# Rope transposes, gate stores, score banks, y tiles, zero tile and raw tiles of y in a two-layer hybrid backbone

## The chip, the cores and the metric

The kernel runs on one core of a Trainium2 chip. The metric is the time of one execution on the device in microseconds (us). Engines are named as in the profile: PE (matmul), PEld (its weight loads), DVE (VectorE), ACT (ScalarE), POOL (GpSimd) and SP (SyncE, which here issues most DMA transfers, in order).

## The reference

Two layers over 1024 latent tokens and 256 context tokens (1280, in ten chunks of 128), model width 1024, all in fp32. Layer 0 runs sixteen neighbourhood-attention heads beside four bidirectional mLSTM heads of width 256, with one input and one output projection. Layer 1 has sixteen bidirectional HGRN2 heads. Each layer is modulated by `c`.

```python
for l in range(DEPTH):
    shift, scale, gate = _ada(c, w_ada[l], b_ada[l])
    h_lat = _rms(x, norm_w[l]) * (1.0 + scale) + shift
    if l % 2 == 0: y_lat, y_ctx = _ab_mixer(...)   # attention heads || mLSTM heads
    else:          y_lat, y_ctx = _c_mixer(...)    # HGRN2 heads
    x = x + gate * y_lat

# mLSTM, one chunk (forward and backward over the chunks)
s   = einsum(q, k) * exp(dmat - m_t)                # scores, decayed
num = einsum(s, v) + carry_w * einsum(q, C)
den = sum(s) + carry_w * einsum(q, n)
h   = num / maximum(abs(den), exp(-m_t))
C   = dec * C + einsum(k * exp(g - m_new), v)       # state; n likewise
# merge, then the output projection
hb  = _rms(hb * sigmoid(ob), h_norm);  yb = hb * silu(zb)
y   = concatenate([ya, yb]) @ w_out
```

q and k of the mLSTM heads are rotated by an axial rope table.

## The kernel before

**Arithmetic.** Each fp32 operand of a dense product is split into a high and a low part: ACT casts the high part (L74), DVE subtracts for the low one (L75), and each product is three matmuls (L127 to L129, in the output projections L771 to L773). PE bounds most stages.

**Order.** The program is written in the Tile framework. A scheduler orders each engine's instructions by its own model of their times; work marked as filler goes in where an engine is thought free, and `issue_after` ties the issue of a DMA to another instruction. Each engine then works through its row of instructions in order, and a tile (a buffer of a tag with so many copies) is written again only when its last reader is done. PSUM has two "mm" and two "tr" banks for the whole program, and further ones for a phase: in the mLSTM recurrence two "s" and two "acc".

**Stages** (times in the trace): norm and modulation to about 50 us; values of the first attention heads to 80; `rope_tables`, `ml_gates`, the modulation of layer 1 and the q projections of two mLSTM heads (`q_plain_t`) to 190; projections done ahead to 420; attention to about 1313; the mLSTM recurrence to 1725, with output-projection pieces (`out_some`) and gate projections as filler; the rest of layer 0's output projection to 1850; layer 1's projections to 2200, its heads to about 3240, its output projection to the end.

**The places that the change touches.**
- `rope_tables` loads the rope rows (SP), transposes them with four small matmuls (L1045, L1046) and copies the result with six ACT instructions. `ml_gates` follows: it loads the gate weights `wgr`, copies them (`wgw`, DVE L329), projects (L347, three groups, each transposed by L354), runs the gate scans on DVE (L382 to L395, ending in `gR` and, by transposes at L403, `gcol`), and stores Gd and mpd and loads mpb back, five DMAs on SP (L408 to L413).
- `wblock` loads a weight slab in pieces of a raw tile `wraw` (L103) and splits each (L74, L75).
- In the recurrence (`ml_all`) `ml_load` loads a chunk, transposes k in a "tr" bank (L434), copies it to mkT (ACT L436), and later computes scores in an "s" bank (L441), copied to mST (ACT L443). A step makes the numerator in "acc" (L496, L506) and two state updates u in the "s" banks (L513), which DVE adds to the state mC (L521, 128x258). `ml_out` transposes a finished chunk of y by two matmuls in a "tr" bank (L560), scales it into `myt` (ACT L561) and stores it by POOL.
- `out_y` loads y for a token tile in two raw tiles (L760, tag `wraw`, three copies, shared with weights) and splits them; `out_tile` multiplies and adds bias, gate and residual on DVE (L805, L807, L808), with `oxh` loaded by SP at L795.
- At the start of layer 0's last projection a zero tile `gzero` is set by DVE (L1500); its first use is in layer 1's heads.

## Time and profile before

| | |
|---|---|
| median of three runs | 3443.36 us (3441.47 to 3443.4) |
| the profiled execution | 3451.55 us, its span 3449.8 us |
| granted PE clock, mean | 0.995 |
| PE waits of the trace, sum | 37 us, and 5.2 us before the first matmul, 3.8 us after the last |

A row of waits reads: the engine, the bank or tile and line that waited, what it waited for, and the total, times and longest. A row of the timeline reads: start and length in us, engine, line, operation, out<-in; in brackets how long the engine stood idle before it, and for what. A window row gives each engine's busy time in a stretch, then the granted clock of PE.

### The profile page before, as it was taken

The numbers are of one execution on the slowest core, as the hardware profiler recorded it, in microseconds if no ns is written. First come the engines' busy times: TensorE is split into PE (matmuls) and PEld (weight loads), VectorE is DVE, ScalarE is ACT, GpSimd is POOL, SyncE is SP. The second block draws the span as 40 slices with busy tenths as digits, with TensorE's granted clock in tenths as the row PEclk, the third lists the DMA queues.
The fourth block names the chain that finished last, engine by engine and source line by source line (L and its number), as shares of the span: only waits on it lengthen the run. The fifth ranks groups of instructions, "written<-read, shape, count | busy, mean of one in ns | idle before, by whom it ended". The sixth has DMA issues, their size and how long they took to land. (4 is left out here: it accounts for less than half of the span.)

```text
span 3449.8 us, 62306 instructions
## 1 busy us (share of the span) xinstructions
PE 3403.7 (99%) x23360; PEld 3065.3 (89%) x23360; DVE 2349.8 (68%) x5814; ACT 1495.6 (43%) x3469; POOL 498.2 (14%) x834
## 2 busy tenths in 40 slices
PE   8999999999999999999999999999999999999999
PEld 5689999999999999987879998899999999999887
DVE  5577757666666654666678666577777777777855
ACT  5322245555544534555546323444444444444431
POOL 3111212222222211211212111000000000000010
PEclk9999999999999999999999999999999999999999
DMA  8543422232223225464473332211111111111345
GB/s 270 185 134 109 127 63 72 69 96 73 81 76 87 77 89 164 143 184 146 137 252 130 110 105 92 77 41 62 53 49 54 61 53 50 56 61 51 114 149 169
DMA packets 359517, 359.62 MB, mean 104 GB/s; under 512 B 30584, under 2 KB 304184, under 8 KB 359088
## 3 DMA queue, kind: packets, MB, share of 16 engines
q1 hardware_dynamic: 315248, 246.36, 24.2%
q0 software_dynamic: 43824, 109.16, 9.2%
q8 instruction: 184, 3.01, 0.4%
q14 instruction: 117, 0.96, 0.1%
q10 hardware_dynamic: 144, 0.13, 0.0%
HBM read 271.98 MB, written 83.42 MB: 103 GB/s over the span
## 5 line engine op out<-in xcount | busy, mean ns | idle before, releaser
L129 PE MATMUL mm<-hh,wl 128*128 128x512 f32 (+1 forms) x1564 | 567.7, 363 | 2.7 <-DVE wl L75 2.7
L127 PE MATMUL mm<-hh,wh 128*128 128x512 f32 (+1 forms) x1564 | 564.3, 361 | 0.3 <-ACT ev L1072 0.2
L128 PE MATMUL mm<-hl,wh 128*128 128x512 f32 (+1 forms) x1564 | 563.9, 361 | 0.0
L127 PE MATMUL mm<-wh,hh 128*128 128x256 f32 x1880 | 541.4, 289 | 1.3 <-ACT wh L74 1.2
L129 PE MATMUL mm<-wh,hl 128*128 128x256 f32 x1880 | 541.7, 289 | 0.2 <-DVE hl L75 0.2
L128 PE MATMUL mm<-wl,hh 128*128 128x256 f32 x1880 | 541.2, 288 | 0.5 <-DVE wl L75 0.3
L127 PEld LDWEIGHTS mm<-wh,hh 128*128 128x128 f32 x1880 | 358.3, 191 | 5.3 <-issue 2.6
L129 PEld LDWEIGHTS mm<-wh,hl 128*128 128x128 f32 x1880 | 358.7, 191 | 4.4 <-issue 2.4
L128 PEld LDWEIGHTS mm<-wl,hh 128*128 128x128 f32 x1880 | 358.6, 191 | 3.0 <-DVE wl L75 1.0
L127 PEld LDWEIGHTS mm<-hh,wh 128*128 128x128 f32 x1564 | 295.6, 189 | 44.2 <-issue 5.1
L129 PEld LDWEIGHTS mm<-hh,wl 128*128 128x128 f32 x1564 | 295.2, 189 | 42.6 <-DVE wl L75 3.1
L128 PEld LDWEIGHTS mm<-hl,wh 128*128 128x128 f32 x1564 | 295.6, 189 | 38.6 <-issue 1.7
L74 ACT CAST wh<-wraw 128x512 fp32r<-128x512 f32 x292 | 179.7, 621 | 266.2 <-PE mm L128 156.9
L1212 ACT COPY gksel<-gK 128x512 f32<-128x512 f32 x224 | 148.6, 664 | 276.9 <-PE s L1221 265.2
L75 DVE TENSOR_TENSOR wl<-wraw,wh 128x512 fp32r<-128x512 f32 x292 | 197.3, 684 | 55.4 <-ACT wh L74 52.8
L1221 PE MATMUL s<-gQ,gksel 128*128 128x128 f32 x1536 | 202.1, 276 | 0.0
L1221 PEld LDWEIGHTS s<-gQ,gksel 128*128 128x128 f32 x1536 | 192.6, 191 | 5.8
L771 PE MATMUL mm<-woh,yh 128*128 128x512 f32 (+1 forms) x420 | 169.8, 404 | 4.9 <-DVE oacc L805 2.5
L773 PE MATMUL mm<-woh,yl 128*128 128x512 f32 (+1 forms) x420 | 164.6, 393 | 0.9 <-DVE yl L75 0.9
L772 PE MATMUL mm<-wol,yh 128*128 128x512 f32 (+1 forms) x420 | 165.3, 394 | 0.0
L1242 DVE TENSOR_TENSOR gQ<-gQ,gT 128x256 f32<-128x256 f32 x384 | 143.1, 413 | 21.2 <-PE s L1221 21.2
L1234 DVE COPY_PREDICATED gA<-glm,s 128x512 f32<-128x512 uint8 x160 | 117.2, 733 | 55.8 <-PE s L1221 55.8
(590 smaller groups left out, 7981.7 us busy)
## 6 DMA issues: line engine op xcount, KB each, us to landing
wraw<-in_wc_dram SPq DMA_DIRECT2D x130, 256.0 KB
wraw<-yd SPq DMA_DIRECT2D x128, 256.0 KB
wraw<-in_wab_dram SPq DMA_DIRECT2D x98, 256.0 KB
md<-ev POOLq DMA_DIRECT2D x78, 256.0 KB, 2.7
adar<-in_wada_dram POOLq DMA_DIRECT2D x16, 1024.0 KB, 6.0
b<-in_wc_dram SPq DMA_DIRECT2D x62, 256.0 KB
adar<-in_wada_dram SPq DMA_DIRECT2D x16, 512.0 KB
wraw<-in_wab_dram SPq DMA_DIRECT2D x64, 128.0 KB
```

The source lines that it names most:

```text
L74: nc.scalar.copy(hi, x)
L75: nc.vector.tensor_tensor(out=lo, in0=x, in1=hi.bitcast(F32), op=ALU.subtract)
L127: mm(ps, lhsT=lh(k), rhs=rh(k), start=(first and k == 0), stop=False)
L128: mm(ps, lhsT=lh(k), rhs=rl(k), start=False, stop=False)
L129: mm(ps, lhsT=ll(k), rhs=rh(k), start=False, stop=(last and k == nk - 1))
L771: mm(ps, lhsT=yh[:, k, :], rhs=w.h(k)[:, cols], start=(k == 0), stop=False)
L772: mm(ps, lhsT=yh[:, k, :], rhs=w.l(k)[:, cols], start=False, stop=False)
L773: mm(ps, lhsT=yl[:, k, :], rhs=w.h(k)[:, cols], start=False, stop=(k == 7))
L1212: nc.scalar.copy(ksel.rearrange("p (b s i) -> p b s i", s=2, i=h), pick(K))
L1221: nc.tensor.matmul(pa[:, c, :].rearrange("p (b s i) -> p b s i", s=2, i=h), lhsT=ksel[:, c * P : (c + 1) * P], rhs=qp[:, c * nbc : (c + 1) ...
L1234: nc.vector.copy_predicated(A, self.lmask[:, lev - 1, :].unsqueeze(1).to_broadcast([P, 4, P]), pa)
L1242: nc.vector.tensor_tensor(out=t[:, i, :, s, :], in0=t[:, i, :, s, :], in1=bc(tot), op=ALU.mult)
```

## The change

Six edits; the matmuls and all other computing instructions are the same in number and kind.

1. `rope_tables` returns a function `turn`, and `ml_gates` calls it after its three projection groups, so the four transposes and six copies come later.
2. `ml_gates` returns a function `store` for the five DMAs of Gd, mpd and mpb. It is called after both `q_plain_t`, with an issue tied to the last weight load.
3. The scores of the mLSTM heads go to the "tr" banks, leaving the "s" banks to the state updates.
4. `myt` has three copies in place of two.
5. `out_y` takes tag and copies of its raw tiles: four `wraw` in layer 0's last projection (the early weights of layer 1 there share them), and six `yraw` of their own in the tail of layer 1.
6. `gzero` and its memset move to the opening of the pool of layer 1's heads.

```diff
@@ -100,7 +100,7 @@
             off = 0
             for s in srcs:
                 c = s.shape[1]
-                nc.sync.dma_start(
+                self.last_w = nc.sync.dma_start(
                     out=r3[:, :, off : off + c],
                     in_=s[i * step * P : (i + 1) * step * P].rearrange("(k p) f -> p k f", p=P),
                 )
@@ -319,7 +319,7 @@
         return self.proj_out(c0, dst, gate, rev)
 
 
-    def ml_gates(self, pool, keep):
+    def ml_gates(self, pool, keep, turn):
         nc, a = self.nc, self.a
         raw = self.t(pool, [P, KD, P], F32, "wgr", 1)
         nc.sync.dma_start(out=raw, in_=a["wg"].rearrange("(k p) f -> p k f", p=P))
@@ -361,6 +361,7 @@
                 nc.scalar.activation(
                     dst[32:36, b0 : b0 + n], ps[q + 64 : q + 68, ::-1], AF.Identity, bias=self.bg[q + 64 : q + 68, :]
                 )
+        turn()
         tmp = self.t(pool, [36, T], F32, "gt", 1)
 
         nc.vector.scalar_tensor_tensor(out=tmp, in0=gf, scalar=-1.0, in1=gf, op0=ALU.mult, op1=ALU.max)
@@ -404,14 +405,18 @@
             p4 = p.rearrange("p m (d x) -> p m d x", x=32)[:, :, :, 0:4]
             nc.vector.tensor_copy(self.gcol[:, c : c + m], p4[:, :, 0:2])
             nc.scalar.activation(self.thr[:, c : c + m], p4[:, :, 2:4], AF.Exp, scale=-1.0)
-        for d in range(2):
-            nc.sync.dma_start(out=self.Gd[d], in_=GG[32 * d : 32 * d + 4, :])
-            nc.sync.dma_start(out=self.mpd[d], in_=mp[32 * d : 32 * d + 4, 0:NT])
         self.mpb = self.t(keep, [P, 2, 4, NT], F32, "mpb", 1)
-        nc.sync.dma_start(
-            out=self.mpb.rearrange("p d h c -> p (d h c)"),
-            in_=self.mpd.rearrange("d h c -> (d h c)").partition_broadcast(P),
-        )
+
+        def store():
+            for d in range(2):
+                nc.sync.dma_start(out=self.Gd[d], in_=GG[32 * d : 32 * d + 4, :])
+                nc.sync.dma_start(out=self.mpd[d], in_=mp[32 * d : 32 * d + 4, 0:NT])
+            nc.sync.dma_start(
+                out=self.mpb.rearrange("p d h c -> p (d h c)"),
+                in_=self.mpd.rearrange("d h c -> (d h c)").partition_broadcast(P),
+            )
+
+        return store
 
 
     def ml_slot(self, h, tt, n):
@@ -436,7 +441,7 @@
         nc.scalar.copy(kT, p)
 
         def score():
-            s = self.ps("s", [P, P])
+            s = self.ps("tr", [P, P])
             for j in range(2):
                 nc.tensor.matmul(s, lhsT=kT[:, j, :], rhs=st["q"][tt][:, j, :], start=(j == 0), stop=(j == 1))
             st["S"][tt] = self.t(pool, [P, P], F32, f"mST{sl}", 2)
@@ -555,7 +560,7 @@
         self.rsqrt(r, ss, 0.25 / 256)
         nc.vector.scalar_tensor_tensor(out=hs, in0=hs, scalar=r, in1=g["z"], op0=ALU.mult, op1=ALU.mult)
         p = self.ps("tr", [P, 2, P])
-        yt = self.t(pool, [P, 2, P], F32, "myt", 2)
+        yt = self.t(pool, [P, 2, P], F32, "myt", 3)
         for j in range(2):
             nc.tensor.transpose(p[:, j, :], hs[:, j * P : (j + 1) * P], self.ident)
             nc.scalar.activation(yt[:, j, :], p[:, j, :], AF.Copy, scale=self.hnb[:, 2 * h + j : 2 * h + j + 1])
@@ -751,11 +756,11 @@
         nc.gpsimd.dma_start(out=self.yd[p2], in_=z)
 
 
-    def out_y(self, tt, q, ysrc, yp, bufs, rp=None):
+    def out_y(self, tt, q, ysrc, yp, bufs, raws=("wraw", 3)):
         yh = self.t(yp, [P, 8, P], F32R, "yh", bufs)
         yl = self.t(yp, [P, 8, P], F32R, "yl", bufs)
         for k in range(0, 8, 4):
-            yr = self.t(rp or yp, [P, 512], F32, "wraw", 3).rearrange("p (j t) -> p j t", j=4)
+            yr = self.t(yp, [P, 512], F32, *raws).rearrange("p (j t) -> p j t", j=4)
             k0 = q * 8 + k
             self.nc.sync.dma_start(
                 out=yr, in_=ysrc[k0 : k0 + 4, :, tt * P : (tt + 1) * P].rearrange("j p t -> p j t")
@@ -1040,6 +1045,15 @@
             nc.sync.dma_start(out=v(rc)[:, :, b, :], in_=rope[0:64, :, 0, 1, :])
         self.roper = self.t(pool, [P, 2, 16], F32, "roper", 1)
         self.ropec = self.t(pool, [P, 2, 64], F32, "ropec", 1)
+
+
+        def turn():
+            self.rope_turn(rr, rc)
+
+        return turn
+
+    def rope_turn(self, rr, rc):
+        nc = self.nc
         p = self.ps("tr", [P, 2, 80])
         for i in range(2):
             nc.tensor.transpose(p[:, i, 0:16], rr[:, i * P : i * P + P], self.ident[0:16, 0:16])
@@ -1420,14 +1434,16 @@
                         self.mod_tr(0, [xts[tt], xts[tt + 1]], tt, pool, self.h_sink(tt * P))
                 self.na_values(0, w)
             with self.pp.phase(ad=2), tc.tile_pool(name="gates", bufs=1) as pool:
-                self.rope_tables(rtp, (pool, "qs", 2))
-                self.ml_gates(pool, mlk)
+                turn = self.rope_tables(rtp, (pool, "qs", 2))
+                store = self.ml_gates(pool, mlk, turn)
                 self.adab, self.adak = 2, 4
                 self.ada_gate(0, pool)
                 self.ada(1, pool)
                 self.ada_gate(1, pool)
                 for h in range(2):
                     self.q_plain_t(h)
+                with tc.issue_after(self.last_w.ins):
+                    store()
             la.close()
             with self.pp.phase(sa=4), tc.tile_pool(name="qa", bufs=1) as pool:
                 self.q_open([(0, 1), (1, 2), (3, 2)], a["wab"], (self.wp, "ev", 2), (self.wp, "wraw", 3), (pool, "qs", 2), 2)
@@ -1496,8 +1512,6 @@
             with tc.tile_pool(name="op0", bufs=2) as op, ExitStack() as wl:
                 wl1 = wl.enter_context(tc.tile_pool(name="wo1", bufs=1))
                 w1 = wo(1, 0, [(wl1, "wo", 8)] * 8)
-                self.zero = self.t(lk, [P, CTX], F32, "gzero", 1)
-                nc.vector.memset(self.zero, 0.0)
                 self.lmask = self.t(lk, [P, 6, P], U8, "glm8", 1)
                 self.lmask0 = self.t(lk, [P, P], F32, "glm0", 1)
                 self.ident8 = self.t(lk, [P, P], U8, "ident8", 1)
@@ -1525,7 +1539,7 @@
                     dma(out=xt[:, 512:D], in_=self.x1[tt * P : (tt + 1) * P, 512:D])
                     part = self.t(op, [P, 512], F32, "og", 3)
                     dma(out=part, in_=self.x1[tt * P : (tt + 1) * P, 0:512])
-                    self.out_tile(w1, 0, tt, self.out_y(tt, 1, self.yd, op, 2), self.xin(tt), xt[:, 0:512], op, part)
+                    self.out_tile(w1, 0, tt, self.out_y(tt, 1, self.yd, op, 2, ("wraw", 4)), self.xin(tt), xt[:, 0:512], op, part)
                     if tt < 8:
                         nc.gpsimd.dma_start(out=self.x1[tt * P : (tt + 1) * P, 0:512], in_=xt[:, 0:512])
                     xn = self.t(op, [P, D], F32, "nx", 2)
@@ -1539,7 +1553,7 @@
                     if tt in (5, 7):
                         k = 512 * len(early)
                         src = a["wc"][k : k + 512, 3 * 2048 : 3 * 2048 + 256]
-                        early.append(self.wblock(self.wp, "w", [src], 4, 256, op, ring=self.slabs))
+                        early.append(self.wblock(self.wp, "w", [src], 4, 256, [op, 4, "wraw"], ring=self.slabs))
 
             with l1:
                 with tc.tile_pool(name="qv", bufs=1) as pool, self.pp.phase(sa=4):
@@ -1556,6 +1570,8 @@
                 sp.close()
                 pool = l1.enter_context(tc.tile_pool(name="hg", bufs=2))
                 self.rawp = pool
+                self.zero = self.t(pool, [P, CTX], F32, "gzero", 1)
+                nc.vector.memset(self.zero, 0.0)
                 l1.enter_context(self.pp.phase(s=3, acc=1))
                 st, parts = self.hg_parts(0, pool, early)
                 for part in sum(parts, []):
@@ -1607,7 +1623,7 @@
                             part = self.t(op, [P, 512], F32, "og", 4)
                             dma(out=part, in_=self.part[tt * P : (tt + 1) * P, :])
                         if b:
-                            ys[tt] = self.out_y(tt, 1, self.yd2, *((yp, 2) if tt < 2 else (op, 6)))
+                            ys[tt] = self.out_y(tt, 1, self.yd2, *((yp, 2) if tt < 2 else (op, 6, ("yraw", 6))))
                         cuts = 0 if b or tt < 7 else 2
                         self.out_tile(w, b, tt, ys[tt], self.x1[tt * P : (tt + 1) * P], xt, op, part, cuts)
                         for c in range(max(1, cuts)):
```

The order of instructions changes over the whole of the gate, projection and mLSTM stages. Line numbers of the changed kernel are higher: L386 for L385, L393 for L392, L439, L446, L518 and L565 for L434, L441, L513 and L560, L765 and L800 for L760 and L795.

DVE in the gate stage, around the weight splits (wl) of the second q head and the last gate operations; before:

```order
L392 COPY gGG_986<-gG_960 4x1024
L394 COPY gGG_986<-gG_960 4x1024
L1026 TENSOR_TENSOR ev_1381<-ev_1381,roper_846 128x512
L385 TENSOR_TENSOR gb_957<-gb_957,gG_960 36x1280
L75 TENSOR_TENSOR wl_1422<-wraw_1424,wh_1423 128x512
L1027 TENSOR_TENSOR ev_1381<-ev_1381,qs_1383 128x512
L75 TENSOR_TENSOR wl_1428<-wraw_1430,wh_1429 128x512
L392 COPY gR_984<-gb_957 4x1024
L393 COPY gR_984<-gb_957 4x256
L394 COPY gR_984<-gb_957 4x1024
L395 COPY gR_984<-gb_957 4x256
```

and in the changed kernel:

```order
L393 COPY gGG_986<-gG_960 4x1024
L395 COPY gGG_986<-gG_960 4x1024
L1029 TENSOR_TENSOR qs_1378<-ev_1376,roper_846 64x512
L386 TENSOR_TENSOR gb_957<-gb_957,gG_960 36x1280
L1030 TENSOR_TENSOR qs_1378<-ev_1376,roper_846 64x512
L75 TENSOR_TENSOR wl_1417<-wraw_1419,wh_1418 128x512
L393 COPY gR_984<-gb_957 4x1024
L394 COPY gR_984<-gb_957 4x256
L395 COPY gR_984<-gb_957 4x1024
L396 COPY gR_984<-gb_957 4x256
L75 TENSOR_TENSOR wl_1423<-wraw_1425,wh_1424 128x512
```

The first split comes after one rope operation fewer (L1026, now L1031, stands behind), and the four gR copies stand between the first and the second split. On PE, the transposes of gR (L403, now L404) come when 6 matmuls from the first that reads the first wl are through, where it was 26.

PE in the mLSTM recurrence where two heads overlap, u in "s", y and scores; before:

```order
L506 MATMUL acc_20486<-mC_18930,mqc_20490 128x258 x2
L560 MATMUL tr_20389<-ident_75,mhs_3826_20061 128x128
L513 MATMUL s_20369<-mvw_20365,mkn_3776_19919 128x258
L441 MATMUL s_20425<-mqT_3902_20284,mkT_20291 128x128 x2
L560 MATMUL tr_20344<-ident_75,mhs_3837_20086 128x128
L560 MATMUL tr_20389<-ident_75,mhs_3826_20061 128x128
L441 MATMUL s_20430<-mqT_3907_20297,mkT_20304 128x128 x2
L513 MATMUL s_20451<-mvw_20449,mkn_3672_19599 128x258
L560 MATMUL tr_20473<-ident_75,mhs_3768_19886 128x128
L496 MATMUL acc_20583<-mv_3901_20280,mSD_20581 128x258
L506 MATMUL acc_20583<-mC_20054,mqc_20587 128x258 x2
L771 MATMUL mm_20534<-woh_20114,yh_20535 128x512
```

and in the changed kernel:

```order
L518 MATMUL s_20367<-mvw_20365,mkn_3776_19919 128x258
L518 MATMUL s_20369<-mvw_20365,mkn_3776_19919 128x258
L565 MATMUL tr_20344<-ident_75,mhs_3837_20086 128x128
L565 MATMUL tr_20389<-ident_75,mhs_3826_20061 128x128
L518 MATMUL s_20451<-mvw_20449,mkn_3672_19599 128x258
L565 MATMUL tr_20344<-ident_75,mhs_3837_20086 128x128
L518 MATMUL s_20453<-mvw_20449,mkn_3672_19599 128x258
L565 MATMUL tr_20389<-ident_75,mhs_3826_20061 128x128
L518 MATMUL s_20496<-mvw_20494,mkn_3667_19586 128x258
L446 MATMUL tr_20425<-mqT_3902_20284,mkT_20291 128x128 x2
L518 MATMUL s_20498<-mvw_20494,mkn_3667_19586 128x258
L446 MATMUL tr_20430<-mqT_3907_20297,mkT_20304 128x128 x2
```

Scores now stand in "tr"; the updates u of one more pair of steps stand in the piece, with no projection matmul between.

SP in the tail of layer 1, loads of y (L760, now L765) and of the residual (L795, now L800) around the last y tiles; before:

```order
L760 DMA wraw_38450<-yd_4_66 128x4x128
L760 DMA wraw_38488<-yd_4_66 128x4x128
L795 DMA oxh_38389<-x_7_69 128x512
L760 DMA wraw_38492<-yd_4_66 128x4x128
L795 DMA oxh_38443<-x_7_69 128x512
L760 DMA wraw_38530<-yd_4_66 128x4x128
L760 DMA wraw_38534<-yd_4_66 128x4x128
L760 DMA wraw_38572<-yd_4_66 128x4x128
L760 DMA wraw_38576<-yd_4_66 128x4x128
L795 DMA oxh_38485<-x_7_69 128x512
```

and in the changed kernel:

```order
L103 DMA wraw_38385<-in_woc_dram 128x512
L103 DMA wraw_38433<-in_woc_dram 128x512
L765 DMA yraw_38492<-yd_4_66 128x4x128
L103 DMA wraw_38439<-in_woc_dram 128x512
L765 DMA yraw_38530<-yd_4_66 128x4x128
L765 DMA yraw_38534<-yd_4_66 128x4x128
L765 DMA yraw_38572<-yd_4_66 128x4x128
L765 DMA yraw_38576<-yd_4_66 128x4x128
L800 DMA oxh_38389<-x_7_69 128x512
L800 DMA oxh_38443<-x_7_69 128x512
```

All loads of y now stand ahead of the residual tile oxh_38389 and those after it, and three weight loads among the last of them.

## The prediction

> **What bounds the kernel now.** I read the page's engine shares first, then TensorE's waits, then the windows for the granted clock, and last the timeline around single stalls.

> ```profile
> span 3449.8 us, 62306 instructions
> PE 3403.7 (99%) x23360; PEld 3065.3 (89%) x23360; DVE 2349.8 (68%) x5814; ACT 1495.6 (43%) x3469; POOL 498.2 (14%) x834
> ```

> TensorE (PE) is busy 3403.7 of 3449.8 us, so it sets the time, and the change adds and removes none of its matmuls. It can win only what PE idles (46.1 us) and what a lowered clock costs; it can lose whatever new waits the new order makes. PE's waits of over 0.1 us that bear on the change or stand beside it (line, what it waited for, total us, times, longest):

> ```profile
> PE mm L771 <- ACT yh L74: 3.9, 5, 2.2
> PE tr L239 <- DVE ntmp L249: 2.8, 3, 1.8
> PE mm L129 <- DVE wl L75: 2.7, 2, 2.5
> PE mm L771 <- DVE oacc L805: 2.5, 2, 1.6
> PE tr L560 <- ACT myt L561: 2.5, 1, 2.5
> PE s L441 <- DVE mC L521: 2.2, 1, 2.2
> PE s L441 <- ACT mST L443: 1.7, 2, 1.5
> PE mm L771 <- issue: 1.2, 1, 1.2
> PE s L441 <- ACT mkT L436: 1.0, 3, 0.4
> PE tr L1045 <- DMA qs<-in_rope_dram: 0.9, 1, 0.9
> PE mm L773 <- DVE yl L75: 0.9, 2, 0.5
> PE tr L1046 <- DMA qs<-in_rope_dram: 0.6, 1, 0.6
> PE mm L347 <- DVE wgw L329: 0.2, 1, 0.2
> ```

> The edits aim at L1045/L1046 (rope transposes), L129 behind wl (gate stage), L441 (scores, 4.9 us in all), L560 (y transposes), and L771/L773 behind oacc and yl (output projections): about 14 us of the 46. A stall can cost more than its idle time. The windows show it (start:end, length, busy us and count for PE, PEld, DVE, ACT, POOL, granted clock, DMA share, GB/s):

> ```profile
> 100.00:150.00 50.00, 47.31 (x260) 33.01 (x261) 35.28 (x64) 15.03 (x25) 8.62 (x13) 1.00 0.57 186
> 250.00:300.00 50.00, 50.00 (x357) 47.28 (x356) 46.76 (x79) 16.89 (x30) 4.14 (x7) 1.00 0.28 84
> 1400.00:1450.00 50.00, 50.00 (x340) 46.53 (x339) 33.82 (x106) 26.90 (x80) 14.71 (x36) 1.00 0.53 166
> 1450.00:1500.00 50.00, 47.45 (x252) 40.93 (x251) 37.30 (x112) 30.37 (x83) 7.18 (x20) 0.97 0.67 201
> 1550.00:1600.00 50.00, 47.58 (x224) 39.71 (x223) 33.53 (x107) 29.27 (x77) 4.91 (x16) 0.97 0.50 150
> 1600.00:1650.00 50.00, 47.27 (x222) 39.19 (x221) 31.57 (x101) 27.89 (x81) 12.81 (x31) 0.97 0.50 152
> 1650.00:1700.00 50.00, 48.10 (x230) 40.23 (x229) 35.56 (x112) 26.03 (x71) 11.06 (x21) 1.00 0.34 106
> 1800.00:1850.00 50.00, 48.16 (x275) 42.29 (x274) 42.59 (x75) 39.52 (x90) 13.18 (x21) 0.97 0.52 166
> ```

> Windows with a stall of 1.8 to 2.5 us mostly show 0.97, which is 0.03 x 50 = 1.5 us of clock lost beside the idle time; the window with 1.5 us (1650) and the one with 2.5 us in the gate stage (100) show 1.00. So I price a stall of about 2 us or more at 1.5 us on top in the mLSTM stage (1313 to 1725 us), and at nothing in the gate stage.

> [...]

> **The change, part by part.** Rope transposes: PE waits 0.9 + 0.6 for the rope rows, before the gate projections (L347). What comes next there:

> ```profile
> 82.73 0.23 DVE L329 COPY wgw<-wgr 128x128 f32<-128x128 f32 x1 [2.56 <-DMA wgr<-in_wg_dram]
> 83.11 1.48 PE L347 MATMUL mm<-hh,wgw 128*32 128x512 f32 x10 [0.22 <-DVE wgw L329]
> ```

> L347 needs wgw, which ends at 82.96 because its load lands then; SP issues that load behind the rope loads both before and after. So L347 still starts near 83.0, and the freed 1.5 us become a wait for wgw. The four transposes move into a full PE stream (0.6 us, priced below by four small matmuls of the same kind), and six ACT copies go with them. I take +0.6; bounds -0.9 (if wgr comes sooner with less beside it) and +1.5 (if the copies delay an ACT eviction that PE awaits).

> Gate stores: their five DMAs leave SP's queue until the weights of the two q heads are issued. But the 2.5 us at L129 end with VectorE, not with SP:

> ```profile
> 131.25 1.48 DVE L385 TENSOR_TENSOR gb<-gb,gG 36x1280 f32<-36x1280 f32 x1
> 132.66 0.68 DVE L75 TENSOR_TENSOR wl<-wraw,wh 128x512 fp32r<-128x512 f32 x1
> 134.57 0.69 DVE L392 COPY gR<-gb 4x1024 f32<-4x1024 f32 x1
> ```

> DVE has no idle time ahead of these; the weight split L75 stands behind L385 and the rest of the gate chain. In the new order one rope operation (0.7) leaves that place, so wl comes 0.7 sooner; but the four gR copies (two of 0.69 and two of a quarter of the columns, an estimate of 0.29 each: 1.95) now stand directly behind it, and PE has their transposes right behind the matmuls that it releases. wl ends near 132.6; gR near 134.6; PE has about six matmuls (1.3 us) between, and reaches the transposes near 133.4: a new wait of 1.2. Sum -0.7 + 1.2 = +0.5; bounds -2.5 (the stall is gone) and +3 (the second split, also behind the copies, is awaited too).

> Score bank and y tile (the mLSTM stage). The scores (L441) leave the two "s" banks, which they share with the state updates u (L513), for the two "tr" banks, which hold the transposes of k (L434) and y (L560). What frees the banks, over that stage:

> ```profile
> L521 DVE SCALAR_TENSOR_TENSOR mC<-mC,mcw,s 128x258 f32<-128x258 f32 x128 | 60.7, 480 | 33.8 <-PE s L513 27.1 <-PE acc L506 6.0
> L561 ACT ACTIVATE myt<-tr,hnb 128x128 f32<-128x128 f32 x79 | 28.0, 362 | 16.0 <-PE tr L560 12.6 <-DMA yd<-myt 3.0
> L436 ACT COPY mkT<-tr 128x256 f32<-128x256 f32 x40 | 14.7, 367 | 5.7 <-PE tr L434 5.6
> L443 ACT COPY mST<-s 128x128 f32<-128x128 f32 x40 | 10.5, 263 | 14.8 <-PE s L441 14.3
> ```

> ```profile
> 1612.80 0.38 PE L513 MATMUL s<-mvw,mkn 128*128 128x258 f32 x1
> 1613.01 0.61 PE L441 MATMUL s<-mqT,mkT 128*128 128x128 f32 x4
> 1615.80 0.37 ACT L561 ACTIVATE myt<-tr,hnb 128x128 f32<-128x128 f32 x1 [3.05 <-DMA yd<-myt]
> 1616.22 0.33 PE L560 MATMUL tr<-ident,mhs 128*128 128x128 f32 x1 [2.49 <-ACT myt L561]
> ```

> The last two rows are the y stall: ACT waits 3.05 us for the store of an older y tile, with only two such tiles; PE waits 2.49 behind it. A third tile lets ACT write at once, and nothing else in that wait is late. Gross gain 2.5 + 1.5 of clock = 4.0. The scores wait 4.9 us, and the largest of those (2.2, window 1550) also has the 0.97: 6.4. Together 10.4.

> What comes back: u keeps "s" alone, but the new order is not looser everywhere. A u spends 0.2 us a pass on PE (0.4 for two), a small matmul 0.11 (the four overlapping ones take 0.61, so 0.11 to 0.15 each). With those, I counted in both orders the places where a bank is taken again within 1.1 us of PE work after its last matmul: 18 before (14 in "s", 4 in "tr"), 18 after (10 and 8). They sit where two heads overlap, as in the piece of PE's order shown above: six u, four y transposes and two scores back to back. There PE spends some 0.65 per u, while DVE owes each 0.48 (L521) beside its other chain. By count alone all 4.9 + 1.5 would come back; but a score then no longer waits behind a u on DVE, and ACT frees its bank in 0.26 to 0.37. Between these I take 2.5 of idle and one clock loss, 4.0, so the net is -6.4. Bounds: -14.1 (nothing comes back, and the 2.2 + 1.5 around 1473, L771 behind yh, go as well) and +16 (the second rival).

> Zero tile and fourth raw tile, output projection of layer 0. In the first row below DVE stands 1.37 us in a memset that reuses memory of the last y tiles:

> ```profile
> 1733.37 0.27 DVE L1500 MEMSET gzero<- 128x256 f32 x1 [1.37 <-DMA yd<-myt]
> ```

> It moves to layer 1's pool, behind that layer's first projection. The waits of PE after it, 0.9 (oacc), 0.9 (yl) and 0.6 (a share of yh), sum to 2.4; they come from DVE being late, but some of them well after it, so I take -1.5. The 1.8 at L239 (around 1841, with clock) hangs on the norm chain, which is untouched. Bounds -5.7 (2.4 and 1.8 + 1.5 all go) and +2.4 (the new order makes as many again).

> Six raw tiles in the tail of layer 1:

> ```profile
> 3378.80 0.33 SPq L795 DMA_DIRECT2D oxh<-x  x1
> 3388.25 0.62 ACT L74 CAST yh<-wraw 128x512 fp32r<-128x512 f32 x1 [2.36 <-DMA wraw<-yd]
> 3388.90 0.69 DVE L75 TENSOR_TENSOR yl<-wraw,yh 128x512 fp32r<-128x512 f32 x1 [2.08 <-ACT yh L74]
> ```

> The last y loads are queued on SP behind an oxh load that waits until 3378.80 for an output store; so the cast starts at 3388.25, the split at 3388.90, and PE's accumulator comes free late: the 1.6 of L771 behind oacc. In the new order the y loads stand ahead of those oxh loads. The oxh loads are then later, but they are added after a tile's eight products. I take -1.6; bounds -2.8 (the 1.2 "issue" goes too) and +1 (an oxh load is now the late one). That 1.2 comes from a gate load that a pool's release holds; it stays.

> Sum: +0.6 + 0.5 - 6.4 - 1.5 - 1.6 = -8.4. The profiled execution took 3451.55 (1.75 around its span), 8.2 above the median of the three; so 3443.2 by its own clock, and 3443.36 - 8.4 = **3435** for the median.

> **The rivals.** *The stalls only form anew elsewhere:* of the mLSTM gains the y wait alone is kept (-2.5), layer 0 gives nothing, the tail -1.6, the front +1.1: -3.0, 3440.4. For it: 18 close reuses before and after. Against: scores and u no longer hold each other up.

> *Slower, by the tr banks:* kT, scores and y now share two banks, 120 tiles in place of 80. Two y tiles are transposed side by side, and while both stand half done no kT or score can start, so the chain score, mST (0.26), mSD, numerator comes late. If each of the 20 pairs (40 y tiles) cost 1.0 us (two ACT evictions of 0.36 and one mST), and four of the waits a clock loss of 1.5, that is 26 against gross gains of 10.4 + 2.0: +13.6, 3457. It decides once new waits pass 12.4 + 6.9, about 19 us. For it: in the new order y pairs stand open across some 25 rows. Against: ACT is busy 27 of 50 us there, and the window at 1400 has no PE idle at all.

> *All of it goes:* mLSTM -14.1, layer 0 -5.7, tail -1.6, front 0: -21.4, 3422. Against it: the close reuses, and the norm chain.

> *The front part does not do what it says* (wgw and DVE bind, not rope and SP): that is in the forecast already.

> **How the numbers follow.** A measurement of this kernel tells no less than about 0.2% (6.9 us, below 3436.5 or above 3450.3). Forecast 0.42 (0.36 of it faster, 0.06 same), stalls anew 0.20 (0.15 same, 0.05 slower by some more of them), tr banks 0.24 (slower), all gone 0.14 (faster). That makes faster 0.50, same 0.21, slower 0.29. The forecast's own range is 3429 to 3440; with "all gone" below and most of the "tr banks" above it becomes 3420 to 3453.

> **What would show it.** Right: no L1045 wait at 80 but about 1.9 before L347; a wait of PE at 133 to 135 for gR or wl; no L560 wait for myt; L441 rows gone and a few u or score waits of 1 to 2 us where heads overlap, with at least one window of 0.97 fewer between 1313 and 1725; no DVE wait in the memset; no PE gap near 3390. Wrong: L441, L434 or L560 waits behind ACT that sum to over 10 us, new 0.97 windows, or a wait in 190 to 420, where DVE's order changes too and DVE, busy 46.76 of 50 us in the window at 250, has little slack.

## The result, and the profile after

| | median us | runs |
|---|---|---|
| before | 3443.28 (3436.56 to 3448.1) | 22 |
| changed | 3437.94 (3434.55 to 3442.77) | 22 |

The ratio is 0.9986, its 95% interval 0.998 to 0.9992: faster by 5.3 us by the medians, between 2.8 and 6.9 us by the interval. That is on the forecast side and inside its range, but the 8.4 us of the sum lie outside the interval, and at 0.16% the gain is inside what I had called no change. Three single executions in the runs below took 4175 us or more; the ratios leave them out.

The profiled execution of the changed kernel took 3440.12 us. The page's first lines:

```profile
span 3438.4 us, 62336 instructions
PE 3398.6 (99%) x23360; PEld 3060.1 (89%) x23360; DVE 2347.2 (68%) x5814; ACT 1498.9 (44%) x3469; POOL 502.9 (15%) x834
```

The same PE waits as shown of before, now (line, what was awaited, total us, times, longest):

```profile
PE s L518 <- DVE mC L526: 3.8, 1, 3.8
PE mm L776 <- ACT yh L74: 3.5, 5, 1.4
PE mm L347 <- DVE wgw L329: 2.7, 1, 2.7
PE mm L127 <- ACT wh L74: 2.4, 1, 2.4
PE mm L129 <- DVE wl L75: 1.8, 1, 1.8
PE tr L127 <- DVE ntmp L249: 1.8, 1, 1.8
...
PE tr L404 <- DVE gR L395: 0.7, 1, 0.7
...
PE tr L446 <- ACT mkT L441: 0.4, 2, 0.3
PE mm L778 <- DVE yl L75: 0.4, 1, 0.4
```

The rope waits, the wait for myt, the waits behind oacc and all but 0.4 us of the score waits are gone. In their place stand a wait of 3.8 us of the state updates (L518, the old L513), one of 2.4 behind a weight's high part, 2.7 behind wgw and 0.7 behind gR. The windows of the mLSTM stage, the gate stage and the tail (columns as before):

```profile
100.00:150.00 50.00, 47.52 (x267) 33.97 (x267) 35.10 (x64) 16.38 (x33) 9.57 (x15) 0.97 0.60 199
1450.00:1500.00 50.00, 46.24 (x273) 41.34 (x272) 32.73 (x103) 27.17 (x69) 9.21 (x19) 0.97 0.54 164
1550.00:1600.00 50.00, 49.81 (x244) 42.04 (x243) 35.57 (x114) 32.90 (x87) 7.57 (x21) 1.00 0.47 143
1600.00:1650.00 50.00, 49.99 (x243) 41.37 (x242) 35.54 (x116) 29.15 (x85) 13.59 (x33) 1.00 0.55 166
3350.00:3400.00 50.00, 50.00 (x214) 39.77 (x214) 30.12 (x47) 11.81 (x19) 4.88 (x9) 1.00 0.70 224
```

From 1550 to 1650 PE has no stall left (before: 47.58 and 47.27 busy at a clock of 0.97). At 1450 it is worse than before (46.24 against 47.45).

The two spans differ by 11.4 us, twice the medians' difference. Where they part can be read to a hundredth: in stages whose order is the same, PE's matmuls keep one constant distance between the two traces. It is +2.0 us at 60 us (+1.8 within the first 20 us, in code that is the same), +3.8 at 490 (after the gate stage), +3.6 at 1300, -7.0 from 1870 to 3200 (after the mLSTM and layer 0's projection), -8.2 at 3290 and -11.4 at the end. Which of these the change makes, the experiments tell.

### The profile page after: what moved, and what is told of

Its sections match the earlier page's. It is cut to its first block, busy times and chain, and to the rows that moved or that the text cites. A ratio compares the mean times of both kernels' runs of the same rounds, so it can differ in the third digit from the quotient of the medians.

```text
span 3438.4 us, 62336 instructions
## 1 busy us (share of the span) xinstructions
PE 3398.6 (99%) x23360; PEld 3060.1 (89%) x23360; DVE 2347.2 (68%) x5814; ACT 1498.9 (44%) x3469; POOL 502.9 (15%) x834
## 5 line engine op out<-in xcount | busy, mean ns | idle before, releaser
L129 PE MATMUL mm<-hh,wl 128*128 128x512 f32 (+1 forms) x1564 | 567.8, 363 | 1.8 <-DVE wl L75 1.8
L129 PE MATMUL mm<-wh,hl 128*128 128x256 f32 x1880 | 541.9, 289 | 0.2 <-DVE hl L75 0.2
L129 PEld LDWEIGHTS mm<-wh,hl 128*128 128x128 f32 x1880 | 358.4, 191 | 3.4 <-issue 1.6
L129 PEld LDWEIGHTS mm<-hh,wl 128*128 128x128 f32 x1564 | 295.8, 189 | 40.8 <-DVE wl L75 2.0
L74 ACT CAST wh<-wraw 128x512 fp32r<-128x512 f32 x292 | 179.8, 621 | 267.3 <-PE mm L128 157.9
L75 DVE TENSOR_TENSOR wl<-wraw,wh 128x512 fp32r<-128x512 f32 x292 | 197.0, 684 | 58.6 <-ACT wh L74 56.4
```

The costliest lines, as they stand in the source:

```text
L74: nc.scalar.copy(hi, x)
L75: nc.vector.tensor_tensor(out=lo, in0=x, in1=hi.bitcast(F32), op=ALU.subtract)
L129: mm(ps, lhsT=ll(k), rhs=rh(k), start=False, stop=(last and k == nk - 1))
```

## The experiments

Each is timed against before in runs beside it; the columns are the medians and the ratio with its 95% interval.

| run | edits | before | this | ratio |
|---|---|---|---|---|
| e1_front | 1, 2 | 3441.85 | 3442.64 | 0.9997 (0.9988 to 1.0006) |
| e2_gate | 2 | 3441.85 | 3441.59 | 1.0001 (0.9992 to 1.001) |
| e3_score | 3 | 3441.85 | 3439.79 | 0.9991 (0.9982 to 1.0) |
| e4_myt | 4 | 3441.85 | 3439.21 | 0.999 (0.9982 to 0.9999) |
| e5_mlstm | 3, 4 | 3443.16 | 3437.84 | 0.9984 (0.9976 to 0.9993) |
| e6_op0 | 6, half of 5 | 3443.16 | 3443.57 | 1.0004 (0.9995 to 1.0013) |
| e7_tail | half of 5 | 3443.16 | 3441.39 | 0.9997 (0.9988 to 1.0006) |
| e8_nofront | 3 to 6 | 3443.16 | 3437.84 | 0.9989 (0.998 to 0.9998) |
| e9_score_again | 3 | 3442.84 | 3435.24 | 0.9981 (0.9972 to 0.999) |
| e10_qpool | 3 to 6, q loads on POOL | 3442.84 | 3433.69 | 0.9977 (0.9967 to 0.9986) |
| e11_wpool | 3 to 6, weights on POOL | 3442.84 | 3435.92 | 0.9982 (0.9973 to 0.9991) |
| e12_qgpool | 3 to 6, q and mGb on POOL | 3442.77 | 3436.74 | 0.9984 (0.9974 to 0.9993) |

The edits sit in different stages, and the program's order shows that they reach no further: with edits 1 and 2 alone PE's rows are those of before from about 305 us on; edit 4 alone leaves them until late in the recurrence; edit 2 alone and the tail edit change none of PE's rows.

**The front part.** Edits 1 and 2, then edit 2 alone (`turn()` called right after `rope_tables`).

```diff
-                self.rope_tables(rtp, (pool, "qs", 2))
-                self.ml_gates(pool, mlk)
+                turn = self.rope_tables(rtp, (pool, "qs", 2))
+                store = self.ml_gates(pool, mlk, turn)
...
+                with tc.issue_after(self.last_w.ins):
+                    store()
```

> Edits 1 and 2 alone (rope transposes after the gate projections, gate stores after the q heads); everything after about 200 us keeps the order of before. The theory of the prediction: the wait for the rope rows turns into one for wgw (about 2 us at L347), the 2.5 us at the first wl shrinks and a wait for gR appears; +1.1 us, between -0.9 and +4.5. What the profile of the full change suggests: +1.8 us up to 490 us, with a half-clock stretch near 135 us. Rival (the edits do what they are made for): both waits go, -4 us.

> Edit 2 alone: the stores of Gd and mpd and the load of mpb leave SP's queue until after the q heads; PE's order is that of before. If SP's queue holds the weight loads up there, the 2.5 us at L129 behind wl shrink by 1 us or more and the time falls by as much. If VectorE's own chain holds wl up (the prediction), the wait stays within 0.7 us of 2.5 and the time within 1 us of before. The difference to the run with edits 1 and 2 is the price of the moved transposes.

Medians: +0.8 and -0.3 us, both within the interval of no change. PE's waits between 75 and 140 us, first of edits 1 and 2, then of edit 2 alone:

```profile
PE mm L347 <- DVE wgw L329: 2.5, 1, 2.5
PE mm L129 <- DVE wl L75: 1.8, 1, 1.8
PE tr L404 <- DVE gR L395: 0.6, 1, 0.6
```

```profile
PE mm L129 <- DVE wl L75: 2.4, 1, 2.4
PE tr L1058 <- DMA qs<-in_rope_dram: 0.9, 1, 0.9
PE tr L1059 <- DMA qs<-in_rope_dram: 0.6, 1, 0.6
PE mm L347 <- DVE wgw L329: 0.6, 1, 0.6
```

With SP's queue freed of the stores (second fence) the wait behind wl is 2.4 as before: SP never held it. With the transposes moved (first fence), the rope waits of 1.5 and the 0.2 to 0.6 behind wgw become 2.5 behind wgw, and 2.4 behind wl becomes 1.8 + 0.6 with gR. The waits only change their names. Between two matmuls that keep their place in the order (77 and 305 us of before) e1_front and the full change both took 229.8 us, with one half-clock stretch each (10 us at 0.83, so 1.7 us lost), where before took 228.0 with none: beside the clock the moved transposes cost nothing that these traces show.

**Score bank and y tile.**

```diff
-            s = self.ps("s", [P, P])
+            s = self.ps("tr", [P, P])
...
-        yt = self.t(pool, [P, 2, P], F32, "myt", 2)
+        yt = self.t(pool, [P, 2, P], F32, "myt", 3)
```

> Edit 3 alone: scores in the tr banks. Theory of the prediction: the waits of L441 in s (4.9 us and one clock loss of 1.5) go and about 4.0 come back, -2.4 us, while the 2.5 us behind myt may stay. Rival that stalls only form anew: 0 within 1 us. Rival of the tr banks: slower by 5 us or more, with waits of scores, kT or y behind ACT.

> Edit 4 alone: three y tiles. PE's order is that of before up to about 1550 us. Theory: ACT's wait of 3.05 us for a y store and PE's 2.5 us behind it go with the clock loss, -4.0 us; scores still wait in s (4.9 us). Rival: the store only moves the wait to another place (the yd store or the s bank), 0 within 1 us.

> Edits 3 and 4 together. If they add up from the single runs (-2.1 and -2.6 us) this gives -4.7; the theory of the prediction says -6.4. If the two cover the same waits (y and score stalls lie in the same places), about -2.6. The profile should have no L441 wait in s and no wait for myt, and of new waits at most 4 us between 1313 and 1725.

> Edit 3 alone once more, for a usable profile: the first one's profiled execution took 8657 us. If the score bank brings about half of the mLSTM gain, 2 to 3 us faster, with the waits of L441 in s gone and one new wait of about 3.8 us of the updates (L513) behind mC near 1484 us, as in the two runs that hold edits 3 and 4. If that new wait belongs to the two edits together, it is not here.

The first run of edit 3 gave -2.1 us, the second, from which the profile is, -7.6; the two intervals overlap between -6.2 and -3.4 us. Edit 4 alone gave -2.6, both together -5.3. The waits of PE between 1313 and 1725 us, of edit 4 alone, and of edit 3 alone (with both they are those of edit 3, 3.8 behind mC and 3.1 behind wh):

```profile
PE mm L771 <- ACT yh L74: 2.0, 1, 2.0
PE s L441 <- ACT mST L443: 1.5, 1, 1.5
PE s L441 <- DVE mC L521: 1.0, 1, 1.0
PE s L441 <- ACT mkT L436: 1.0, 3, 0.4
PE mm L127 <- ACT wh L74: 1.0, 1, 1.0
...
```

```profile
PE s L513 <- DVE mC L521: 3.6, 1, 3.6
PE mm L127 <- ACT wh L74: 2.9, 1, 2.9
PE tr L441 <- ACT mkT L436: 0.4, 2, 0.3
```

Edit 4 takes away the 2.5 behind myt and nothing else. Edit 3 takes away the score waits and, by the new order, the wait for myt too, though it has two y tiles (second fence): the two edits cover the same wait, and do not add up there. Nothing came back where two heads overlap; no u, k, y or score waits over 0.3 us at a time there. What edit 3 brings instead are the 3.6 to 3.8 behind mC and the 2.9 to 3.1 behind wh, where before had 2.2 (L771 behind yh) and 1.2.

**Layer 0's last projection and the tail.**

```diff
-                self.zero = self.t(lk, [P, CTX], F32, "gzero", 1)
-                nc.vector.memset(self.zero, 0.0)
...
-... self.out_y(tt, 1, self.yd, op, 2), ...
+... self.out_y(tt, 1, self.yd, op, 2, ("wraw", 4)), ...
...
-... ((yp, 2) if tt < 2 else (op, 6)) ...
+... ((yp, 2) if tt < 2 else (op, 6, ("yraw", 6))) ...
```

> Edits 6 and the layer-0 half of 5 alone (zero tile set in layer 1's pool, four raw tiles in layer 0's last projection). Theory of the prediction: -1.5 us, the waits of PE after the memset (2.4 us in before) down by about that. Rival: VectorE is late there for the sake of the loads, not of the memset: 0 within 1 us and the same waits in other rows.

> The tail half of edit 5 alone: six raw tiles of their own; PE's order is that of before. Theory of the prediction: the 1.6 us of PE behind oacc near 3390 go, -1.6 us. Rival, from the runs with edits 1, 2 and 4, whose tails have the order of before and no such wait, or 0.6 us of it: that wait comes in some executions only, so the median moves by less than 0.5 us.

> The full change without edits 1 and 2. If the front part costs (prediction +1.1 us, the two profiles +1.8) this is the fastest, 1 to 2 us below the full change, so about -6 to -7 us against before. If the front edits are free, the same as the full change (-5.3).

Zero tile and fourth raw tile, measured together: +0.4 us (interval -1.7 to +4.5, so the time alone does not rule out the -1.5). VectorE's waits between 1725 and 1800 us tell more, first of this run, then of the full change:

```profile
DVE ident L1502 <- DMA yd<-myt: 1.2, 1, 1.2
```

```profile
...
DVE ident L1518 <- DMA x<-ox: 4.9, 1, 4.9
```

The wait of the memset (1.4 us, for the store of y) is now that of the instruction behind it, the copy of the identity: for the same store and 1.2 us long in this run, for another store and 4.9 us long in the full change. PE's waits that the prediction counted there (oacc, yl, yh) sum to 2.2 us in this run, to 2.4 in before and to 1.7 in e7_tail, which has no such edit.

Tail: -1.8 us by the medians, within the interval. The 1.6 behind oacc and the 1.2 "issue" of before have no successor with the edit, but none either in the tails of e1_front and e2_gate, which keep the old buffers: from layer 1's last score to the end it took 151.7 us in the profiled execution of before, 148.2 and 148.1 in those two, 148.6 with the edit and 148.4 in the full change. That wait came in one execution (e4_myt, with the old buffers too, has 0.6 us of it); the edit earns nothing that these runs can tell.

Without edits 1 and 2 the change gives -5.3 by the medians, as with them.

**The new wait at the projection's start.** Around 1485 us in the profile of the full change (start, length, engine, line, in brackets the idle time before and its cause; SP's queue first):

```profile
1462.83 9.90 SPq L435 DMA_DIRECT2D mqT<-md  x3
...
1475.37 0.33 SPq L103 DMA_DIRECT2D wraw<-in_woab_dram  x1
1477.20 0.80 SPq L820 DMA_DIRECT2D gbc<-gated  x2
...
1478.56 0.86 SPq L103 DMA_DIRECT2D wraw<-in_woab_dram  x2
```

```profile
1483.92 0.62 ACT L74 CAST woh<-wraw 128x512 fp32r<-128x512 f32 x1 [3.60 <-DMA wraw<-in_woab_dram]
...
1484.57 0.69 DVE L75 TENSOR_TENSOR wol<-wraw,woh 128x512 fp32r<-128x512 f32 x1 [2.94 <-ACT woh L74]
1485.18 0.48 DVE L526 SCALAR_TENSOR_TENSOR mC<-mC,mcw,s 128x258 f32<-128x258 f32 x1
...
1485.71 1.75 PE L518 MATMUL s<-mvw,mkn 128*128 128x258 f32 x4 [3.76 <-DVE mC L526]
```

The named releaser, mC, stands on DVE behind a weight split, that behind ACT's cast, and that behind a weight load which SP issued late. On SP loads of q stood ahead, waiting for scores. Three kernels, all without edits 1 and 2, took the suspects from SP's queue:

```diff
-        nc.sync.dma_start(out=q, in_=self.md[("q", h)]...
+        nc.gpsimd.dma_start(out=q, in_=self.md[("q", h)]...
```

> The full change without edits 1 and 2, and the loads of q in the recurrence (40, ml_load) issued by POOL instead of SP. Theory: the 3.8 us wait near 1484 comes because a load of q on SP waits for scores that now come later, and the output-projection weights queue behind it; with q on another queue that wait goes with its clock loss of 1.7, 5.5 us less than without (about 3432). Rival: the weights are late for other loads as well, no gain; or POOL, which then carries 40 issues of some 0.75 us, delays the y stores and norms, slower.

> The same base, but the weight loads of the work beside the recurrence (gate projections of head 3, output projection) issued by POOL, the loads of q on SP as they were. Theory: as in the run with q on POOL, the wait near 1484 goes (about 3432); also the 2.4 to 3.2 us near 1347 behind wh, whose load queues on SP behind 22 recurrence loads, goes: about 3428. Rival: 48 more issues on POOL hold up its y stores, and waits for myt come back: no gain or slower.

> As the run with q on POOL, and the loads of mGb (the other recurrence load that waits for scores, 20.5 us on SP in that run) on POOL too. Theory: SP then has nothing in front of the output-projection weights that waits for a late score; the first of them is issued 5 us or more before the last matmul of the gate projections instead of about 2 us, the wait of 3.6 us of the updates behind mC near 1478 goes with its clock loss, 3 to 5 us less than with q alone on POOL (3429 to 3431). Rival: that wait hangs on the memory of the projection input, which is free only when the last gate projection has read it; then it stays. Second rival: POOL, blocked in a load that waits for a score, holds up norms and y stores: slower.

The waits of PE between 1313 and 1725 us with q on POOL, and with q and mGb on POOL:

```profile
PE s L513 <- DVE mC L521: 3.6, 1, 3.6
...
```

```profile
PE acc L496 <- ACT mhs L535: 3.8, 1, 3.8
PE s L513 <- DVE mC L521: 0.5, 1, 0.5
...
```

My theory fell: the wait behind wh (2.7 in e8_nofront, their base) is gone in both, but the one at the projection's start stays, 3.6 and 3.8, and with the weights themselves on POOL it is 5.0, behind a y load that SP still carries. With q and mGb on POOL, SP issues like this, and ACT waits all the same:

```profile
1461.71 1.45 SPq L103 DMA_DIRECT2D wraw<-in_woab_dram  x2
1463.32 0.80 SPq L815 DMA_DIRECT2D gbc<-gated  x2
1464.21 0.38 SPq L103 DMA_DIRECT2D wraw<-in_woab_dram  x1
...
1465.99 1.43 SPq L103 DMA_DIRECT2D wraw<-in_woab_dram  x1
...
1471.78 0.62 ACT L74 CAST woh<-wraw 128x512 fp32r<-128x512 f32 x1 [4.25 <-DMA wraw<-in_woab_dram]
```

The weight that ACT casts at 1471.78 was issued at 1464.21, over 7 us before it landed; in the full change the load behind the cast at 1483.92 was issued at 1478.56 and took 5 us. Nine weight loads, six of y and the two gate rows go out within 20 us of the change of work, and in the run with q and mGb on POOL the DMA engines are mostly at eight tenths of busy or more from 1463.5 to 1475 us (at nine tenths or more in every half microsecond from 1469 on). So I take the start of the projection to be limited by this burst, before (2.2) as now; that transfers and not one queue set it is argued from that share, and no run moved the burst itself.

The condition of the last theory did not come about either: the first of these loads goes out at 1461.71, not 5 us but 1.6 us before the last matmul of the gate projections ends, although SP had issued nothing since 1449.0. Four of the first six weight loads (1461.71, 1462.83, 1465.99, 1473.15) start 0.02 to 0.03 us after DVE ends a weight split (L75, at 1461.68, 1462.81, 1465.96 and 1473.12), so they seem to wait for one of the three raw tiles. More raw tiles there is the rival that no run tested.

With q on POOL the kernel is the fastest of all, 3433.69 us, 0.9977 of before, where the full change is 0.9986. The intervals of these two ratios overlap, so it beats before clearly and the changed kernel only by the medians.

## Why the prediction was right, point by point

**Right side, right range.** The forecast of 3435 was 2.9 us low; the sum of -8.4 came out as -5.3. By the medians of the single runs the difference lies in the two small terms, but neither of these is told from 0. Of the 0.42 for the forecast 0.36 stood for a gain of over 6.9 us, and that did not come.

**Front, +1.1:** the mechanisms named all came (wgw in place of rope, DVE and not SP behind wl, a new wait for gR): 0.7 us of gR against the 1.2 expected, 1.8 of wl against 1.8. The medians say +0.8, not to be told from 0. The price did not come as reckoned: I had put the clock at nothing in the gate stage, but a wait of 2.45 us for wgw in e1_front and one of 1.83 for wl in the full change were each followed by 10 us at 0.83, and these 1.7 us are nearly all of the +1.8 between 60 and 490 us. One sign of being wrong came with it, a new window of 0.97 (100 to 150 us). That the +1.8 lies near the +1.1 is luck.

**mLSTM, -6.4:** held within its size: -5.3 for both edits (interval -2.4 to -8.3). PE's idle time from the first numerator to the last was 11.2, 10.7, 9.4, 8.8 and 10.1 us in the five profiled executions that have the old order there (before, e1_front, e2_gate, e6_op0, e7_tail), and is 6.6, 7.4 and 7.0 in the full change, e5_mlstm and e8_nofront. From a matmul at 1312 us of before to one at 1870, both in stretches of common order, the same five took 558.1, 551.8, 548.4, 551.7 and 549.2 us and these three 547.4, 548.6 and 546.4: 4.3 us less by the medians, for the mLSTM and the rest of layer 0's projection together, where the two terms had 7.9. But the reason for the discount was wrong. I took 4.0 us to come back where heads overlap, by counting 18 close reuses of a bank before and after. None came back there. It came back at the two starts of filler work that I had put down as untouched: 2.2 became 3.8 at the projection's start, 1.2 became 2.4 behind wh. That these 2.8 us are about the 2.5 of idle time that I had discounted elsewhere is luck.

**Layer 0's projection, -1.5:** the step that failed. "They come from DVE being late", and the memset was taken for the cause of that; it was only the first in line at memory that a store still holds (1.4 us in before), and the next instruction waited in its place (1.2 us in e6_op0). Measured +0.4, with PE's waits there at 2.2 us in place of 2.4.

**Tail, -1.6:** the step was mis-sized because it was read from one execution. In other executions of the same order the wait is absent, or 0.6 us.

**The sum against one execution.** The profile of before was 8.2 us above the median, and I subtracted without asking why. It had lost more clock than others: the windows with its stalls at 1473, 1560 and 1616 all showed 0.97. In e7_tail, whose order there is that of before, the same stalls cost none:

```profile
1450.00:1500.00 50.00, 47.48 (x259) 40.85 (x258) 38.09 (x116) 29.68 (x81) 6.68 (x22) 1.00 0.71 212
1550.00:1600.00 50.00, 48.34 (x234) 40.59 (x233) 34.97 (x111) 30.01 (x78) 5.49 (x18) 1.00 0.52 161
1600.00:1650.00 50.00, 47.45 (x233) 39.57 (x232) 33.39 (x107) 28.50 (x82) 13.02 (x31) 1.00 0.50 151
```

In the five executions of the old order these two stalls of the mLSTM term (scores near 1560, y near 1616) lost clock in three of ten cases (10 us at 0.83), so their 3.0 us were worth less on the median. Behind the wait of 3.6 to 5.0 us at the projection's start clock was lost in all seven executions that have it (0.71 to 0.83 over the next 10 us).

**The rivals.** "Slower, by the tr banks" did not come: the only wait on scores is 0.4 behind mkT. "Stalls anew" was nearer to the number (3440.4) than to the place. "All of it goes" did not come.

## What to carry to other kernels

A wait's name is the last link: before pricing its removal, ask what stands second, for here the rope wait (1.5 us) became wgw's (2.5), the memset's (1.4) became the next copy's (1.2), and the wait for myt (2.5) went with those for the scores (4.9). Read stalls of one to two us from several executions of the same order before paying for an edit; the tail's price and the clock losses here came from one. Where two kinds of tile with different readers shared banks, parting them by reader emptied a stage of stalls here (4.9 us of waits on scores became 0.4), and the gain was then bounded, as argued, by the loads at the next change of work.

## What the runs showed of the hardware

Not every stall of PE cost clock beside its idle time. Taken over thirteen profiled executions, the 10 us after each PE wait of over 1.2 us (from 60 us on) showed a granted clock of 1.00, or of 0.83 or less (0.83 is 1.7 us lost; three of the longest showed 0.71 or 0.72):

| wait of PE | waits | with clock lost |
|---|---|---|
| 1.2 to 1.8 us | 23 | 1 |
| 1.8 to 2.6 us | 30 | 13 |
| over 2.6 us | 11 | 9 |

Length alone did not part them in these runs: in before a wait of 2.47 us (behind wl, until 133.39) was followed by 10 us at 1.00, and one of 1.16 us (behind wh, until 1345.92) by half clock from 1347.41 to 1350.82.

```profile
1470.29:1473.70 3.41, 1.24 (x6) 0.74 (x5) 1.79 (x7) 2.00 (x6) 0.00 (x0) 1.00 1.07 374
1473.70:1477.12 3.42, 3.42 (x10) 2.67 (x9) 3.42 (x12) 3.42 (x9) 0.00 (x0) 0.50 1.06 319
```

```profile
1471.32:1474.73 3.41, 2.89 (x16) 2.24 (x14) 0.83 (x5) 0.60 (x3) 0.00 (x0) 1.00 0.89 245
1474.73:1478.15 3.42, 2.06 (x9) 1.81 (x10) 3.19 (x12) 2.99 (x9) 0.00 (x0) 1.00 1.08 366
```

In before the whole stall of 2.17 us lies in one step and the next runs at half clock; in e7_tail the 1.87 us are parted into 0.52 and 1.36, and nothing is lost.
